# A hybrid attention layer on one core: the order of small work at four joints, and a last row block in column halves

## Chip, core and metric

One NeuronCore of a Trainium2 chip runs the whole layer. The metric is the device time of one execution in microseconds, from runs on the chip; shorter is better.

## The reference, cut to what matters

A single encoder layer in float32 over 1024 tokens of width 1024: a half-step SwiGLU, attention, and a second half-step SwiGLU, each between two RMS norms. One projection gives q, k and v; eight heads attend over a two-dimensional neighbourhood, eight over a mixture of dilated windows; each group is normalised and the two go through one output matrix.

```
h = swiglu(rmsnorm(x, ffn1_pre_g[l]), ffn1_w_gate[l], ffn1_w_up[l], ffn1_w_down[l])
x = x + 0.5 * rmsnorm(h, ffn1_post_g[l])
h = rmsnorm(x, mix_pre_g[l])
qkv = (h @ w_qkv[l]).reshape(B, S, 3, N_HEADS, HEAD_DIM).transpose(2, 0, 3, 1, 4)
...
o_na = rmsnorm(o_na.transpose(0, 2, 1, 3).reshape(B, S, D_NA), na_out_g[l])
o_dil = rmsnorm(o_dil.transpose(0, 2, 1, 3).reshape(B, S, D_DIL), dil_out_g[l])
mixed = jnp.concatenate([o_na, o_dil], axis=-1) @ w_out[l]
x = x + rmsnorm(mixed, mix_post_g[l])
h = swiglu(rmsnorm(x, ffn2_pre_g[l]), ffn2_w_gate[l], ffn2_w_up[l], ffn2_w_down[l])
x = x + 0.5 * rmsnorm(h, ffn2_post_g[l])
```

## The kernel before, in words

**Arithmetic.** Every large product is made from high and low parts of both factors: ScalarE casts a high part, VectorE subtracts it to get the low part, and TensorE does three matmuls (high by high, high by low, low by high). The feed-forward products and the q, k and v projections go by a seven-product scheme over halves of the matrices (`PASSES`, line 31), in which a pass may go on accumulating in the banks of the pass before it (`CHAINED`, line 32).

**What sets the order.** The program writes TensorE's order out by hand. Small work of the other engines is handed out in between. `c.todo` is a queue of closures of which one is popped at each `c.tick()`, and `c.steps` and `c.sums` are queues of which one entry each is popped at each `c.step()`, which stands every few matmuls. `plan(n, {i: [...]})` fills `c.todo` with n ticks and what is to run at each. `c.behind(f, engine)` places what f issues behind the latest instruction of that engine. Apart from such ties, VectorE and ScalarE are put into an order when the program is built, by what is ready and by the order in which it was written. On the chip every engine runs its own list strictly in order.

**Row blocks.** The 1024 tokens are eight blocks of 128 rows, t = 0 to 7, of which 0 to 3 and 4 to 7 are the two halves of the scheme. `fin.rest` adds the normalised result of a sub-layer to x (line 892), stores x and hands the block to `op.norm`, which takes squares on ScalarE (`sumsq`, line 166), a reciprocal root on VectorE (`rstd_of`, lines 149 to 159) and a scaling (line 230). `op.put(t)` transposes a block on TensorE (line 174) and builds the scheme's operands from it (`left_half`, `right_half`, lines 290 to 319).

**The values joint.** `vp.run(0, 1)` does two passes of the value projection in twelve ticks: eight of two chunks for one row block each, then four of four chunks. The plan for it has blocks 4 and 5 at tick 0, the transposes of block 4 at tick 8 and blocks 6 and 7 at tick 10. After it `pg.ahead` starts the q and k projection: product of pair 0, a copy of it out of its bank (`save` and `keep`, line 488), product of pair 1, then a second product of pair 0 on top of the first in the same bank.

**The local heads.** Eight neighbourhood heads (`na_head`) of eight steps each follow the eight dilated heads, with a tick at every second step. In their first ticks the last pair of dilated heads is finished. `merge` (line 1255) reads `obn`, which comes back from memory, weighs two partial results on VectorE, has GpSimd multiply (lines 1281 and 1282) and VectorE add (line 1285). Then `attended` (line 1862), which only the last pair has as its `then`, queues the norm of the dilated rows: squares, root, scaling (line 1390) and transposes into the operand of the output projection, and between them `begin`, which puts matmuls of the output projection between the steps of the heads.

**The output joint.** After the last head, the norm of the neighbourhood rows is finished and they are transposed, eight blocks in two quads, among sixteen matmul groups: a closure of `puts` after the groups 2, 3, 5, 6, 9, 10, 12 and 13. `GroupNorm.put` (line 1392) makes four transposes (line 1401) into one of two banks, and for each of two strips a cast on ScalarE (line 1405) and a subtraction on VectorE (line 1406).

**The tail.** In the last pass of the last feed-forward layer eleven chunks are added up for the row blocks 4 to 7 in turn (line 793). `combine` adds the bank to what is kept (line 830), `Finish.half` takes the squares and multiplies by the gain (line 850), `Finish.end` makes the root (lines 864 to 867 and `newton`, lines 322 to 329) and adds the scaled result to x in two halves (line 871), one stored from SP's queue and one from ScalarE's (line 872). The right halves of these blocks are complete one pass earlier.

Of the kernel before, what the change touches and what calls it, by code (L numbers as in the profile page):

```python
# [22 lines left out]
EPS = 1e-6  # L23
# [706 lines left out]
class Passes:  # L730
# [4 lines left out]
    def __init__(self, c, n, left, right, take, last=None):  # L735
        self.c, self.left, self.right, self.take = c, left, right, take
        self.own = not isinstance(left, Operand)
        groups = [list(range(i, min(i + 4, n))) for i in range(0, n, 4)]
        self.groups = [groups] * 6 + [last or groups]
        self.groups[0] = [groups[0][:2], groups[0][2:]] + groups[1:]  # L740
        self.todo = deque((p, g[j:j + 2]) for p in range(7) for g in self.groups[p] for j in range(0, len(g), 2))
        self.ready = deque()
# [27 lines left out]
    def run(self, *which, upto=6):  # L770

        c = self.c
        for p in which:
# [4 lines left out]
            for gi, g in enumerate(groups):  # L778
                self.fetched(len(g) + 1, upto)
                ops = [self.ready.popleft() for _ in g]  # L780
                end = gi == len(groups) - 1
                for t in range(4):
                    if t == 1:
                        self.fetched(3, upto)
                    if acc[t] is None:
                        acc[t] = c.psm.tile([P, T], F32, tag="mm", name="accp")
                    sl = slice(t * P, (t + 1) * P)
                    n = 2 if t == 0 else 1
                    for j in range(0, len(ops), n):
                        two = [(a[:, sl], b) for i in (0, 1, 2) for (ahi, alo), (bhi, blo) in ops[j:j + n]  # L790
                               for a, b in [((ahi, bhi), (alo, bhi), (ahi, blo))[i]]]
                        for i, (a, b) in enumerate(two):
                            c.nc.tensor.matmul(acc[t], a, b, start=not chained and gi == 0 and j == i == 0,  # L793
                                               stop=end and j + n >= len(ops) and i == len(two) - 1,
                                               skip_group_check=chained)
                        if n == 2 or j % 2:
                            c.step()
                    if end:
                        self.take(p, t, acc[t])
                    c.tick()  # L800


def combine(c, halves, rows):
# [7 lines left out]
    def take(p, t, ps):  # L811
# [17 lines left out]
        else:  # L829
            nc.vector.tensor_add(c21[:, t], ps, c21[:, t])  # L830
            halves(4 + t, 0, c21[:, t])
            rows(4 + t, second[:, t])
    return take


class Finish:


    def __init__(self, c, src, dst, gain, op, last=False):
        self.c, self.src, self.dst, self.gain, self.op, self.last = c, src, dst, gain, op, last  # L840
        self.ss = c.small.tile([P, 8, 2], F32, tag="fss", name="fss", bufs=1)
        self.xs = {}

    def half(self, t, g, h):

        sumsq(self.c, h, self.ss[:, t, g:g + 1])
        to = h
        if self.last and t >= 4 and g == 0:
            to = self.part = self.c.xp.tile([P, T], F32, tag="hm", name="hm")
        self.c.nc.vector.tensor_mul(to, h, self.gain[:, g * T:(g + 1) * T])  # L850

    def load(self):
# [4 lines left out]
        self.q = c.small.tile([P, 4], F32, tag="q", name="q", bufs=1)  # L857
        c.behind(lambda: c.nc.scalar.activation(self.q[:, 0:1], c.ident[:, :1], AF.Sqrt), ACT)

    def end(self, t, h):  # L860

        c, nc = self.c, self.c.nc
        x, q = self.xt[t - 4], self.q[:, t - 4:t - 3]
        nc.vector.tensor_scalar(q, self.ss[:, t, 1:2], 0.5 / D, 0.5 * EPS, op0=ALU.mult, op1=ALU.add)
# [4 lines left out]
        for g, queue in enumerate((nc.sync, nc.scalar)):  # L869
            sl = slice(g * T, g * T + T)  # L870
            nc.vector.scalar_tensor_tensor(x[:, sl], h[:, sl] if g else self.part, r, x[:, sl], op0=ALU.mult, op1=ALU.add)  # L871
            queue.dma_start(self.dst[t][:, sl], x[:, sl])
# [238 lines left out]
class DilPair:  # L1111
# [97 lines left out]
    def outs(self, hd, part, quad, un, pt, po):  # L1209
# [30 lines left out]
        if (hd, part, quad) == (1, 0, 1):  # L1240
            c.todo.extend([lambda: None] + [lambda: c.behind(self.merge, DVE, ACT)])
# [13 lines left out]
    def merge(self):  # L1255
# [100 lines left out]
class GroupNorm:  # L1356
# [35 lines left out]
    def put(self, i):  # L1392
# [7 lines left out]
        for j in range(4):  # L1400
            nc.tensor.transpose(ps[:, j, :], o[:, j * P:(j + 1) * P], c.ident)
        for hf in range(2):
# [3 lines left out]
            nc.vector.tensor_sub(lo, src, hi.bitcast(F32))  # L1406


def layer(tc, a, out):
    nc = tc.nc  # L1410
    c = Ctx(tc)
    with ExitStack() as ctx:
# [81 lines left out]
        def ffn(which, op, prep, pg, get, turns, sums, more, post, pre, src, dst, begin=None, tables=()):  # L1494
# [60 lines left out]
            ps.take = combine(c, fin.half, rows)  # L1555
# [70 lines left out]
        with ExitStack() as order:  # L1626
# [142 lines left out]
            def vearly(p, t, ps):  # L1769
# [4 lines left out]
                else:  # L1774
# [9 lines left out]
                      9: [lambda: c.behind(lambda: pg.split_left(0), DVE, ACT)], 10: [A(6, 7)]})  # L1784
# [77 lines left out]
        def attended():  # L1862
# [14 lines left out]
            c.todo.extend(single + [scales[0], lambda: None] + puts[:4] + [begin] + squares + [scales[1], lambda: None])  # L1877
# [18 lines left out]
        with ordered():  # L1896
# [159 lines left out]
```

## Time and profile before

| | us |
|---|---|
| three runs, median | 1828.5 |
| three runs, lowest to highest | 1827.25 to 1829.3 |
| the profiled execution, its own time | 1826.53 |
| the profiled execution, its span | 1824.7 |
| TensorE busy | 1807.9 |
| VectorE busy | 1308.9 |
| ScalarE busy | 831.6 |
| GpSimd busy | 348.8 |

The span runs from the first to the last instruction of the program on the core, and the time holds the 1.8 us around it. An engine counts as busy from the start of an instruction to its end. Matmuls overlap, so TensorE's busy time says little about how densely it works; the distance from one start to the next does. A bracket at the end of a row of a timeline holds the idle time before the instruction and what ended it.

### The profile page before, as it was taken

To read this page: it belongs to the slowest core of one execution; us is meant where nothing else is said; L and a number is where in the kernel's file an instruction comes from. 1 tells how busy PE (TensorE), PEld (TensorE's weight loads), DVE (VectorE), ACT (ScalarE), POOL (GpSimd) and SP (SyncE) were. 2 spreads that over 40 slices of the span, in tenths; PEclk is the share of its full clock that TensorE was granted. 3 is DMA by queue.
4 is the path that set the end of the run, shared out by engine and by line. 5 is a ranking of instruction groups with operands and counts; after the bars stand their busy time and mean duration, and the time that the engine had idled before them with its cause. 6 is when DMAs were issued, how large, how long until landed. Compare 5 with 4: busy or idle time off the path is not lost. (4 is left out here: it accounts for less than half of the span.)

```text
span 1824.7 us, 25161 instructions
## 1 busy us (share of the span) xinstructions
PE 1807.9 (99%) x8876; PEld 1521.7 (83%) x8876; DVE 1308.9 (72%) x2225; ACT 831.6 (46%) x1495; POOL 348.8 (19%) x579
## 2 busy tenths in 40 slices
PE   8999999999999999999999999999999999999998
PEld 6888888888888888888999998887888888888886
DVE  6888877776466877577676856778877777664557
ACT  7522233334534556234688765554223333354433
POOL 2124421112021123232344100221111111110000
PEclk9999999999999999999999999999999999999999
DMA  8756566557888867768687523594655566596564
GB/s 295 258 170 220 171 230 224 193 209 268 307 305 294 288 206 266 261 230 292 193 271 255 183 88 116 193 312 159 197 180 194 201 220 224 184 351 198 191 229 146
DMA packets 172769, 409.28 MB, mean 224 GB/s; under 512 B 20401, under 2 KB 42321, under 8 KB 170594
## 3 DMA queue, kind: packets, MB, share of 16 engines
q1 hardware_dynamic: 125168, 248.68, 41.5%
q0 software_dynamic: 46608, 157.41, 23.7%
q8 instruction: 70, 1.15, 0.3%
q10 hardware_dynamic: 866, 1.58, 0.2%
q14 instruction: 57, 0.47, 0.1%
HBM read 280.09 MB, written 132.56 MB: 226 GB/s over the span
## 5 line engine op out<-in xcount | busy, mean ns | idle before, releaser
L472 PE MATMUL mmp<-x,whi 128*128 128x512 f32 (+1 forms) x1464 | 571.7, 391 | 1.1 <-ACT x L181 0.7
L473 PE MATMUL mmp<-x,whi 128*128 128x512 f32 (+1 forms) x1464 | 569.1, 389 | 0.7 <-DVE x L182 0.7
L793 PE MATMUL accp<-pw 128*128 128x512 f32 x1800 | 411.1, 390 | 0.0
L793 PEld LDWEIGHTS accp<-pw 128*128 128x128 f32 x1800 | 337.2, 188 | 70.0 <-ACT hb L814 0.3
L478 PE MATMUL mmp<-x,wlo 128*128 128x512 f32 (+1 forms) x1464 | 390.5, 388 | 0.2 <-DVE wlo L463 0.2
L472 PEld LDWEIGHTS mmp<-x,whi 128*128 128x128 f32 x1464 | 275.7, 188 | 58.7 <-ACT s L488 1.4
L473 PEld LDWEIGHTS mmp<-x,whi 128*128 128x128 f32 x1464 | 275.7, 188 | 57.2 <-DVE x L182 1.4
L478 PEld LDWEIGHTS mmp<-x,wlo 128*128 128x128 f32 x1464 | 274.4, 188 | 57.4 <-DVE wlo L463 0.6
L761 DVE TENSOR_TENSOR pw<-praw,pw 128x1024 fp32r<-128x1024 f32 (+1 forms) x181 | 200.1, 1143 | 125.6 <-ACT pw L760 124.8
L760 ACT CAST pw<-praw 128x1024 fp32r<-128x1024 f32 (+1 forms) x181 | 168.7, 983 | 207.7 <-PE accp L793 167.3
L462 ACT CAST whi<-wraw 128x1024 fp32r<-128x1024 f32 x126 | 132.6, 1053 | 187.4 <-PE mmp L473 157.9
L463 DVE TENSOR_TENSOR wlo<-wraw,whi 128x1024 fp32r<-128x1024 f32 x126 | 153.9, 1222 | 2.9 <-ACT whi L462 2.9
L703 POOL DMA_DIRECT2D g<-sg x44 | 23.9, 544 | 427.6 <-DVE sg L696 246.5
L462 ACT CAST whi<-traw 128x512 fp32r<-128x512 f32 x52 | 32.3, 621 | 122.6 <-DVE traw L564 89.7
L488 ACT COPY s<-mmp 128x512 f32<-128x512 f32 x49 | 28.8, 588 | 127.7 <-PE mmp L478 121.1
L655 DVE TENSOR_TENSOR c<-mmp,u 128x512 f32<-128x512 f32 x52 | 35.9, 691 | 70.9 <-PE mmp L478 70.7
L563 DVE TENSOR_TENSOR wraw<-wraw 128x1024 f32<-128x1024 f32 x52 | 63.6, 1224 | 17.7 <-DMA wraw<-in_wu_dram 17.0
L793 PE MATMUL accp<-pw,x 128*128 128x512 f32 x312 | 71.8, 390 | 0.0
L1095 DVE CUSTOM_DVE_ANT_0 s<-sp,g 128x256 f32<-128x256 f32 (+1 forms) x128 | 48.4, 413 | 30.7 <-PE sp L1192 24.6
L793 PEld LDWEIGHTS accp<-pw,x 128*128 128x128 f32 x312 | 58.3, 188 | 12.4 <-DVE pw L761 0.3
L642 DVE TENSOR_TENSOR c<-mmp,v 128x512 f32<-128x512 f32 x52 | 35.8, 689 | 34.0 <-PE mmp L478 34.0
L1341 PE MATMUL po<-vs,pt 128*128 128x128 f32 x352 | 49.9, 276 | 0.4 <-DVE pt L1107 0.4
(281 smaller groups left out, 2485.7 us busy)
## 6 DMA issues: line engine op xcount, KB each, us to landing
praw<-g SPq DMA_DIRECT2D x70, 512.0 KB
wraw<-in_wg_dram SPq DMA_DIRECT2D x44, 512.0 KB
wraw<-in_wu_dram SPq DMA_DIRECT2D x44, 512.0 KB
tr<-in_wd_dram SPq DMA_DIRECT2D x44, 512.0 KB
g<-sg POOLq DMA_DIRECT2D x88, 256.0 KB, 5.4
ts<-tr POOLq DMA_DIRECT2D x22, 1024.0 KB, 4.7
praw<-ts SPq DMA_DIRECT2D x88, 256.0 KB
praw<-in_wd_dram SPq DMA_DIRECT2D x66, 256.0 KB
```

Of the source, the lines that this page charges most:

```text
L462: nc.scalar.copy(hi, raw)
L463: nc.vector.tensor_sub(lo, raw, hi.bitcast(F32))
L472: mm(out, hi[:, i, sl], xhi[:, k, cols], start=not go_on and k == 0, stop=False, skip_group_check=go_on)
L473: mm(out, hi[:, i, sl], xlo[:, k, cols], start=False, stop=False, skip_group_check=go_on)
L478: mm(out, lo[:, i, sl], xhi[:, k, cols], start=False, stop=k == 3, skip_group_check=go_on)
L563: nc.vector.tensor_sub(r[:, 0:2], r[:, 1:3], r[:, 0:2])
L655: c.behind(lambda: nc.vector.tensor_add(c21, d, u2), *((DVE,) if self.sink.soon and b == self.n - 1 else ()))
L760: nc.scalar.copy(hi, raw[:, :m])
L761: nc.vector.tensor_sub(lo, raw[:, :m], hi.bitcast(F32))
L793: c.nc.tensor.matmul(acc[t], a, b, start=not chained and gi == 0 and j == i == 0, stop=end and j + n >= len(ops) and i == len(two) - 1, sk ...
L1095: c.nc.vector.tensor_tensor_reduce(out=s, in0=ps, in1=bias, scale=-1.0, scalar=3e38, op0=ALU.add, op1=ALU.min, accum_out=neg)
L1341: nc.tensor.matmul(po[0][:, u], pt[0][:, j, :], vs[:, k0 + j, :], start=j == 0, stop=j == n - 1)
```

## The change

The change has five parts.

1. In the plan of the values joint, blocks 6 and 7 go from tick 10 to tick 7.
2. For the last pair of dilated heads, `merge` is queued behind two empty ticks instead of one, and `attended` runs in the tick of the sum instead of the tick after it.
3. In `attended` an empty tick is put between the root of the first quad and its first transposes.
4. In `GroupNorm.put` with strips, both casts of a block come ahead of both subtractions; in the output joint the root of the second quad is issued ahead of the first block's transposes instead of behind them.
5. In the last pass, block 7 takes its last two chunks apart from the others. The long part is added to what is kept as before; then six matmuls of 256 columns give the left half of the rest in a bank of its own, and six more the right half. Each half is added, squared and multiplied by the gain as it comes, and the left half's mean joins the right half's mean of the pass before, as a bias (`q`) of the square root. For blocks 4 to 7 the square root reads the sum of squares directly, and the Newton step is written as one fused operation between two reciprocals. Block 7's gain products for the left half and for the third quarter of the columns lie in PSUM. VectorE scales and adds these three quarters, and GpSimd does the last quarter with a product and a sum, stored from SP's queue.

```diff
+                    tail = self.tail if end and p == 6 and t == 3 and self.tail else None
+                    rest = ops[-2:] if tail else []
+                    ops = ops[:len(ops) - len(rest)]
...
+                    for i in range(2 if tail else 0):
+                        ps, cols = c.psm.tile([P, T], F32, tag="mm", name="accq")[:, :T // 2], slice(i * T // 2, (i + 1) * T // 2)
+                        six = [(x[:, sl], y[:, cols]) for k in (0, 1, 2) for (ahi, alo), (bhi, blo) in rest
+                               for x, y in [((ahi, bhi), (alo, bhi), (ahi, blo))[k]]]
+                        for k, (x, y) in enumerate(six):
+                            c.nc.tensor.matmul(ps, x, y, start=k == 0, stop=k == len(six) - 1)
+                        tail(i, cols, ps)
...
+    def tail(i, cols, ps):
+        h = c21[:, 3, cols]
+        c.behind(lambda: nc.vector.tensor_add(h, ps, h), DVE)
+        halves(7, -i, h)
+        if i:
+            rows(7, second[:, 3])
...
+        elif g == 1:
+            sumsq(c, h, self.ss[:, 7, 1:2])
+            self.right = c.pst.tile([P, 4, P], F32, tag="tr", name="hr").rearrange("p k x -> p (k x)")[:, :H]
+            mul(self.right, h[:, :H], self.gain[:, T:T + H])
+            mul(h[:, H:], h[:, H:], self.gain[:, T + H:])
+            self.centre(7)
+        else:
+            if g:
+                self.mean(7, 0)
+            else:
+                self.part = c.pst.tile([P, 4, P], F32, tag="tr", name="hl").rearrange("p k x -> p (k x)")
+            cols = slice(-g * H, (1 - g) * H)
+            sumsq(c, h, self.ss[:, 4 if g else 7, 0:1])
+            mul(self.part[:, cols], h, self.gain[:, cols])
...
-        nc.vector.scalar_tensor_tensor(v, self.ss[:, t, 0:1], 0.5 / D, q, op0=ALU.mult, op1=ALU.add)
-        nc.scalar.activation(e, v, AF.Sqrt, scale=2.0)
-        r = newton(c, y, e, v)
...
+        nc.scalar.activation(e, ss, AF.Sqrt, scale=0.25 / D, bias=q)
+        nc.vector.scalar_tensor_tensor(v, ss, 0.25 / D, q, op0=ALU.mult, op1=ALU.add)
+        nc.vector.reciprocal(y, e)
+        nc.vector.scalar_tensor_tensor(e, v, y, e, op0=ALU.mult, op1=ALU.add)
+        nc.vector.reciprocal(y, e)
...
+        out(nc.sync, slice(0, T), self.part)
+        if t < 7:
+            out(nc.scalar, slice(T, D), h[:, T:])
+            return
+        m = T + T // 2
+        out(nc.scalar, slice(T, m), self.right)
+        nc.gpsimd.tensor_mul(h[:, m:], h[:, m:], y.broadcast_to([P, D - m]))
+        nc.gpsimd.tensor_add(x[:, m:], h[:, m:], x[:, m:])
+        nc.sync.dma_start(self.dst[t][:, m:], x[:, m:])
...
-            c.todo.extend([lambda: None] + [lambda: c.behind(self.merge, DVE, ACT)])
+            c.todo.extend([lambda: None] * (2 if self.then else 1) + [lambda: c.behind(self.merge, DVE, ACT)])
...
-        c.todo.extendleft(([self.then] if self.then else []) + [lambda: c.behind(add, DVE), lambda: None,
-                          lambda: c.behind(products, POOL)] + ([] if self.then else [lambda: None]))
+
+        def added():
+            c.behind(add, DVE)
+            if self.then:
+                self.then()
+        c.todo.extendleft([added, lambda: None, lambda: c.behind(products, POOL)] +
+                          ([] if self.then else [lambda: None]))
...
+        lows = []
         for hf in range(2):
...
             nc.scalar.copy(hi, src)
-            nc.vector.tensor_sub(lo, src, hi.bitcast(F32))
+            lows.append((lo, src, hi.bitcast(F32)))
+        for args in lows:
+            nc.vector.tensor_sub(*args)
...
-                      9: [lambda: c.behind(lambda: pg.split_left(0), DVE, ACT)], 10: [A(6, 7)]})
+                      9: [lambda: c.behind(lambda: pg.split_left(0), DVE, ACT)], 7: [A(6, 7)]})
...
-            c.todo.extend(single + [scales[0], lambda: None] + puts[:4] + [begin] + squares + [scales[1], lambda: None])
+            c.todo.extend(single + [scales[0], lambda: None, lambda: None] + puts[:4] + [begin] + squares + [scales[1], lambda: None])
...
-                        puts.append(lambda n=n: (n.put(0), c.behind(lambda: early[1].scale(2), DVE)))
+                        puts.append(lambda n=n: (c.behind(lambda: early[1].scale(2), DVE), n.put(0)))
```

## Rows read from the trace of the kernel before

**Rows 1.** The profile's page, part 1: busy time by engine.

```profile
PE 1807.9 (99%) x8876; PEld 1521.7 (83%) x8876; DVE 1308.9 (72%) x2225; ACT 831.6 (46%) x1495; POOL 348.8 (19%) x579
```

**Rows 2.** The waits of TensorE, whole span: us in total, times, longest.

```profile
PE gps L350 <- DMA xn<-in_ffn_pre_g_dram: 5.6, 1, 5.6
...
PE trp L1401 <- DVE og L1390: 0.4, 1, 0.4
PE trp L174 <- DVE og L1390: 0.4, 1, 0.4
PE po L1341 <- DVE pt L1107: 0.4, 1, 0.4
```

**Rows 3.** Groups of instructions by line and shape: busy us, mean ns, idle before.

```profile
L793 PE MATMUL accp<-pw 128*128 128x512 f32 x1800 | 411.1, 390 | 0.0
...
L1406 DVE TENSOR_TENSOR n<-trp,n 128x256 fp32r<-128x256 f32 x16 | 6.5, 421 | 1.9 <-ACT n L1405 1.9
...
L128 POOL TENSOR_TENSOR wlo<-wraw,whi 128x256 fp32r<-128x256 f32 x16 | 11.6, 729 | 17.1 <-ACT whi L127 17.1
```

**Rows 4.** Timeline, TensorE and ScalarE at 679 to 684 us: start, length, instruction.

```profile
678.95 1.07 PE L478 MATMUL mmp<-x,wlo 128*128 128x512 f32 x4
...
680.77 0.60 PE L174 MATMUL trp<-ident,x 128*128 128x128 f32 x4
681.12 0.48 PE L472 MATMUL mmp<-x,whi 128*128 128x512 f32 x1
...
683.06 0.60 PE L174 MATMUL trp<-ident,x 128*128 128x128 f32 x4
683.78 0.50 PE L472 MATMUL mmp<-x,whi 128*128 128x512 f32 x1
...
681.62 1.06 ACT L166 ACTIVATE junk<-x 128x1024 bf16<-128x1024 f32 x1
...
683.14 0.59 ACT L488 COPY s<-mmp 128x512 f32<-128x512 f32 x1
```

**Rows 5.** Timeline, TensorE and VectorE at 1009 to 1012 us.

```profile
1011.63 0.94 PE L1341 MATMUL po<-vs,pt 128*128 128x128 f32 x6 [0.40 <-DVE pt L1107]
...
1009.48 0.18 DVE L1261 TENSOR_TENSOR mn<-sa,obn 128x16 f32<-128x16 f32 x1 [0.95 <-DMA obn<-rg]
```

**Rows 6.** Timeline, TensorE at 1037 us.

```profile
1036.77 0.63 PE L174 MATMUL trp<-ident,og 128*128 128x128 f32 x4 [0.42 <-DVE og L1390]
```

**Rows 7.** Timeline, TensorE, VectorE and ScalarE at 1112 to 1119 us.

```profile
1113.34 0.40 PE L365 MATMUL accp<-whi,o 128*128 128x512 f32 x1
1113.82 0.63 PE L1401 MATMUL trp<-ident,og 128*128 128x128 f32 x4
...
1118.21 0.63 PE L1401 MATMUL trp<-ident,og 128*128 128x128 f32 x4 [0.43 <-DVE og L1390]
...
1113.60 0.15 DVE L147 TENSOR_TENSOR v<-gss 128x4 f32<-128x4 f32 x1
...
1112.85 0.65 ACT L1405 CAST n<-trp 128x256 fp32r<-128x256 f32 x2 [1.23 <-DVE n L1406]
```

**Rows 8.** Timeline, the end: VectorE and the issue of the last store.

```profile
1816.02 0.75 DVE L871 SCALAR_TENSOR_TENSOR xl<-hb,y,xl 128x512 f32<-128x512 f32 x1
...
1817.35 0.69 DVE L830 TENSOR_TENSOR hb<-accp,hb 128x512 f32<-128x512 f32 x1 [0.59 <-PE accp L793]
...
1818.89 0.16 DVE L866 SCALAR_TENSOR_TENSOR v<-fss,q 128x1 f32<-128x1 f32 x1
...
1819.91 0.16 DVE L328 SCALAR_TENSOR_TENSOR y<-e,y 128x1 f32<-128x1 f32 x1
...
1821.55 0.34 ACTq L872 DMA_DIRECT2D out_dram<-xl  x1
```

**Rows 9.** Timeline, TensorE at 20 us: matmuls of 256 columns.

```profile
19.88 0.64 PE L478 MATMUL mmp<-x,wlo 128*128 128x256 f32 x4
20.35 0.28 PE L472 MATMUL mmp<-x,whi 128*128 128x256 f32 x1
```

More of the change, by code (lines that the diff above doesn't have):

```diff
@@ L740, in __init__ @@
         self.groups[0] = [groups[0][:2], groups[0][2:]] + groups[1:]
+        self.tail = None
         self.todo = deque((p, g[j:j + 2]) for p in range(7) for g in self.groups[p] for j in range(0, len(g), 2))
@@ L799, in run, with combine @@
                         self.take(p, t, acc[t])
+                    for i in range(2 if tail else 0):
[5 more added lines that the diff above has]
+                        tail(i, cols, ps)
                     c.tick()
-def combine(c, halves, rows):
+def combine(c, halves, rows, split=False):
     nc = c.nc
@@ L830, in take @@
             nc.vector.tensor_add(c21[:, t], ps, c21[:, t])
+            if split and t == 3:
+                return
             halves(4 + t, 0, c21[:, t])
             rows(4 + t, second[:, t])
-    return take
+    def tail(i, cols, ps):
[4 more added lines that the diff above has]
+            rows(7, second[:, 3])
+    return (take, tail) if split else take
 class Finish:
@@ L841, in __init__, with mean @@
         self.ss = c.small.tile([P, 8, 2], F32, tag="fss", name="fss", bufs=1)
+        if last:
+            self.q = c.small.tile([P, 4], F32, tag="q", name="q", bufs=1)
         self.xs = {}
     def half(self, t, g, h):
[L846 to L850, printed above, removed]
+        c, nc, H = self.c, self.c.nc, T // 2
+        mul = nc.vector.tensor_mul
+        if not (self.last and t == 7):
+            sumsq(c, h, self.ss[:, t, g:g + 1])
+            to = h
+            if self.last and t >= 4 and g == 0:
+                to = self.part = c.xp.tile([P, T], F32, tag="hm", name="hm")
+            mul(to, h, self.gain[:, g * T:(g + 1) * T])
+        elif g == 1:
[12 more added lines that the diff above has]
+            mul(self.part[:, cols], h, self.gain[:, cols])
+    def mean(self, t, i):
+        q = self.q[:, t - 4:t - 3]
+        self.c.nc.vector.scalar_tensor_tensor(q, self.ss[:, t, i:i + 1], 0.25 / D, q, op0=ALU.mult, op1=ALU.add)
     def load(self):
@@ L856, in load @@
             c.nc.sync.dma_start(self.xt[t], self.src[4 + t])
-        self.q = c.small.tile([P, 4], F32, tag="q", name="q", bufs=1)
         c.behind(lambda: c.nc.scalar.activation(self.q[:, 0:1], c.ident[:, :1], AF.Sqrt), ACT)
@@ L862, in end, with out, centre @@
         c, nc = self.c, self.c.nc
-        x, q = self.xt[t - 4], self.q[:, t - 4:t - 3]
-        nc.vector.tensor_scalar(q, self.ss[:, t, 1:2], 0.5 / D, 0.5 * EPS, op0=ALU.mult, op1=ALU.add)
-        v, y, e = [c.small.tile([P, 4], F32, tag=i, name=i)[:, :1] for i in ("v", "y", "e")]
-        nc.vector.scalar_tensor_tensor(v, self.ss[:, t, 0:1], 0.5 / D, q, op0=ALU.mult, op1=ALU.add)
-        nc.scalar.activation(e, v, AF.Sqrt, scale=2.0)
-        r = newton(c, y, e, v)
[L869 to L872, printed above, removed]
+        x, q, ss = self.xt[t - 4], self.q[:, t - 4:t - 3], self.ss[:, t, 0:1]
+        if t < 7:
+            self.centre(t)
+        else:
+            ss = self.ss[:, 4, 0:1]
+        v, y, e = [c.small.tile([P, 4], F32, tag=i, name=i)[:, :1] for i in ("v", "y", "e")]
+        nc.scalar.activation(e, ss, AF.Sqrt, scale=0.25 / D, bias=q)
[3 more added lines that the diff above has]
+        nc.vector.reciprocal(y, e)
+        def out(queue, cols, src):
+            nc.vector.scalar_tensor_tensor(x[:, cols], src, y, x[:, cols], op0=ALU.mult, op1=ALU.add)
+            queue.dma_start(self.dst[t][:, cols], x[:, cols])
+        out(nc.sync, slice(0, T), self.part)
+        if t < 7:
+            out(nc.scalar, slice(T, D), h[:, T:])
+            return
+        m = T + T // 2
[3 more added lines that the diff above has]
+        nc.sync.dma_start(self.dst[t][:, m:], x[:, m:])
+    def centre(self, t):
+        self.c.nc.vector.tensor_scalar(self.q[:, t - 4:t - 3], self.ss[:, t, 1:2], 0.25 / D, 0.25 * EPS,
+                                       op0=ALU.mult, op1=ALU.add)
     def scale(self, t0, n):
@@ L1554, in rows @@
                     fin.end(t, hs[t])
-            ps.take = combine(c, fin.half, rows)
+            if pre is None:
+                ps.take, ps.tail = combine(c, fin.half, rows, True)
+            else:
+                ps.take = combine(c, fin.half, rows)
             if masks:
```

## The prediction

> **What bounds the kernel now.** I read the busy times first: TensorE is busy 99% of the span, VectorE 72%, the others less [rows 1]. No other engine can be the bound as a whole, so the change can win only where TensorE stands still, and after its last matmul. Second, the list of TensorE's waits [rows 2]: 5.6 us before its first matmul, which the change does not touch, and then three single waits of 0.4 us, each on VectorE. Third, how tightly the matmuls follow one another: 1800 of 512 columns cover 411.1 us, one each 0.228 us, while one takes 0.390 us from start to end [rows 3]. So a matmul normally starts 0.16 us before its predecessor ends. A gap that the profile shows as 0.40 us therefore costs 0.56 us, and a wait of up to 0.16 us shows no gap at all. Fourth, the timelines around those waits and at the end.
>
> These rows limit the matter before any detail: three waits of under 0.6 us, a few hidden ones, and an end in which 4.2 us pass from the last product's first use (1817.35) to the issue of the last store (1821.55) [rows 8]. Over 4 us cannot well come of it, and 0.2% of the time, about what a measurement of this kernel can tell from no change, is 3.7 us.
>
> **Part 1: rows 6 and 7 normalised three ticks earlier (value projection).** In `pg.ahead` the second projection of pair 0 accumulates on top of the first, so it must wait until ScalarE has copied the first out (L488). The bank was complete at 680.0, where the four low-part matmuls end, yet the copy runs only at 683.14 to 683.73, because ScalarE is in the two squares of x rows 6 and 7 (the second ends at 682.7). Four transposes are normally followed by a matmul 0.35 us after they start (680.77 to 681.12); here it takes 0.72 (683.06 to 683.78) [rows 4]. The stall is 0.37 us. From tick 7 the squares are released during the second pass instead, before this copy is due. Everything they bring moves with them: two additions, two stores of x on GpSimd's queue, the root (12 small VectorE operations), the scaling of row 6. The loads and additions have no tie and are ready either way; I cost their move at nothing, since the values pass has no TensorE wait in rows 2 that would show them as late. What is behind the moved work is the split of row 4's sums. Its last step frees the buffer that row 5's copy needs, in ScalarE's queue ahead of L488. I take 0.30 saved. Ends: 0.37 saved, and up to 3.8 us lost (rival 4).
>
> **Part 2: the last merge one tick later.** VectorE reaches the merge at 1009.48 after standing 0.95 us for the load of `obn`; the softmax operations and the copy of the transposed weights queue behind it, and TensorE then waits 0.40 us for that copy [rows 5], so 0.56 us. Two no-ops instead of one move the merge back by one tick, two of the local head's eight steps, and the load has landed by then. The merge's own small operations still cost what they cost, but without a blocked queue. GpSimd's products move one tick later with it; the sum and `attended` fall together into the tick in which `attended` ran, so the squares behind it do not move. I take 0.55 saved. Ends: 0.56 saved; 0.3 lost, if sum and merge meet a fuller stretch of VectorE.
>
> **Part 3: one more no-op ahead of the first transposes of the dilated rows.** At 1036.77 TensorE waits 0.42 us for VectorE's scaling of `og` [rows 6], 0.58 us in all. One tick later that scaling is long done. All following transposes and the filler matmuls also move one tick; their number is unchanged, and fillers only stand elsewhere. I take 0.58 saved. Ends: 0.58 and 0.3, if a filler lands badly.
>
> **Part 4: the output joint.** Two edits act together. The root for the second quad now goes to VectorE before the first transposed block is split: so far its first operation starts at 1113.60, after that split, and TensorE waits 0.43 us at 1118.21 for the row that it scales [rows 7]: 0.59 us. That first subtraction ended as ScalarE was released at 1112.85 and began 0.42 sooner; the root can take its place, about 1.2 us earlier. And both ScalarE copies of a block now precede both VectorE subtractions. So far the second copy waits for the first subtraction: ScalarE idles 1.23 us before it, released by VectorE. That holds the transposes' bank: the third block's transposes start 0.48 us after the matmul before them instead of 0.24 [rows 7], a hidden wait of 0.24. Against it: the subtractions of the first block now share VectorE with the root, which can hold the same bank longer. I take the 0.59 and two thirds of the 0.24: 0.75 saved. Ends: 1.1 (a few tenths more of hidden waits at the later blocks) and nothing.
>
> **Part 5: the tail.** Step by step from the last rows [rows 8]:
> - Matmuls: the last two chunks are six of 512 columns, 6 x 0.228 = 1.37 us; now twelve of 256. Four of these start within 0.47 us (19.88 to 20.35), 0.118 each, and one lasts 0.28 [rows 9]: 1.41 us, and the last one drains 0.11 us sooner. TensorE ends about where it did; the left half is done 0.7 us sooner.
> - VectorE: the addition of the long part is ready 1.4 us before the end, but the engine is in the end of row block 6 until 1816.77 [rows 8]. Block 6's root loses two dependent steps of about 0.2 us (v before the square root, one Newton step), so it is free near 1816.37. Then 0.69 (long addition), and with 256-column operations of 0.42 [rows 3] the left addition, left product and right addition follow, overlapping a little: the right half is ready at about 1818.25. Square and accumulator took the 0.85 us from 1818.04 to 1818.89 at 512 columns; at half, between 0.43 and 0.85, I take 0.55: 1818.80, only 0.1 sooner than now.
> - Root: square root (0.2), reciprocal, one fused step, reciprocal, each 0.2 apart (five steps from 1818.89 to 1819.91 now): y at about 1819.6, against 1820.07 (1819.91 + 0.16).
> - Scaling: VectorE lets go of the left half after 0.67 (its scalings of 512 columns last 0.75 and overlap a little) and needs under 0.5 for a quarter, ready for the ScalarE queue at 1820.8. GpSimd needs two operations of 128x256. The nearest row is 0.729 each [rows 3]: 1819.65 + 1.46 = 1821.1, and SP's queue, whose left-half store was issued at about 1820.4, is free. The last issue is near 1821.15, now 1821.55.
>
> By the GPSIMD Reference of the Trainium skill (section 4.1, engine selection) element-wise work belongs on VectorE, GpSimd being about twice as slow with two inputs. By that, an estimate, each would take 0.84 and the tail would save 0.2; no run here shows that ratio at this size, and the measured 0.729 is used.
>
> I take 0.4 saved; the smaller last transfer is counted as nothing. Ends: 0.8 (GpSimd as fast as VectorE) and 0.7 lost (rival 1). The extra work on block 7's right half one pass earlier (two products of 0.42 instead of one of 0.69, one small step) stands beside TensorE's matmuls, with no wait of TensorE there in rows 2.
>
> **Sum.** 0.30 + 0.55 + 0.58 + 0.75 + 0.4 = 2.6 us. The profiled execution took 1826.5 us (span 1824.7), so 1823.9 for one like it; it was 2.0 us below the median of the three runs, and against that median, 1828.5, the forecast is 1825.9.
>
> **Rivals.**
> 1. *GpSimd sets the end.* If its two operations run only after VectorE's scalings (1820.8), the last store is issued at 1820.8 + 1.46 = 1822.3, 0.7 later than now: the sum is 2.2 - 0.7 = 1.5 saved, 1827.0. For it: both read the same tiles from the same moment. Against: the products that VectorE scales now lie in PSUM. The page SBUF — State Buffer of the Trainium skill (Who interferes with whom) says that a VectorE instruction with two SBUF inputs and a GpSimd one that reads SBUF shut each other out; by it there is no clash here, and no row before shows the pair. Chance 0.12.
> 2. *The stalls move.* VectorE is 72% busy overall [rows 1], so a cured wait may return as the next late copy; if half of parts 1 to 4 comes back, 1.1 + 0.4 = 1.5 saved, 1827.0. The hidden waits (no gap below 0.16 us) speak for it, the fact that each shown wait has one plain cause against. Chance 0.17.
> 3. *All at its best end*: 0.37 + 0.56 + 0.58 + 1.1 + 0.8 = 3.4, and with a shorter last transfer near 3.8: 1824.7. Chance 0.13.
> 4. *Slower: row 6's root ahead of row 4's split.* Twelve steps 0.2 apart and a scaling of 1024 columns (twice the 0.67 to 0.75 of 512) enter VectorE's queue ahead of the last splits of row 4; if all 3.8 us reach the buffer that row 5's copy waits for, ScalarE's copies behind it and TensorE stand for it: 2.3 - 3.8 = 1.5 lost, 1830.0. It decides as soon as the delay exceeds the 2.3 us of the other parts. Against: VectorE is not full, so some of it falls into gaps, and the same work stood behind those splits before. Chance 0.06.
> 5. *No effect on the order*: VectorE and ScalarE are ordered when the kernel is built, and ticks may not change what they do; then only part 3 and the tail count, 1.0 saved, 1827.5. Chance 0.05.
>
> The forecast has the remaining 0.47.
>
> **How the numbers follow.** The range must hold the cases but for 2 in 10, and the three runs before lay 2 us apart: 1823.9 to 1828.2. Faster by over 0.2% (below 1824.8) takes rival 3 and the upper edge of the forecast: 0.18. Slower by over 0.2% would take a stall in the profile that I do not see, or rival 4 and more: 0.03. Within 0.2%: 0.79.
>
> **What would show it.** Right: the three waits of 0.4 us gone from TensorE's list; the copy of pair 0 near 680; no 0.95 us before the merge; the last issue 0.4 us nearer to the last matmul. Wrong: a new wait of TensorE at the values joint, or after the output joint's first block; GpSimd's two operations starting after VectorE's; a TensorE gap between the two halves at the end.

## The result, and the profile after

The change makes the kernel slower: 1833.1 us (median of 10 runs, 1828.2 to 1834.7) against 1828.0 us (10 runs, 1824.3 to 1831.3) of the kernel before. The ratio is 1.0032, 95% interval 1.0024 to 1.0040, so 5.9 us (4.4 to 7.3) by the ratio and 5.1 us by the medians. The forecast was 1825.9 us with a range up to 1828.2. The profiled execution of after took 1833.6 us (span 1831.8), 7.1 us over that of before.

The waits of TensorE come first, as in [rows 2] and without the 5.6 us at the start, which are the same. Line numbers differ in the kernel after: the transposes of the output joint are L1468 (were L1401), the subtractions L1476 (L1406), the scalings of `og` L1457 (L1390).

```profile
PE trp L1468 <- DVE n L1476: 3.7, 1, 3.7
PE mmp L478 <- DVE wlo L463: 1.2, 1, 1.2
PE po L1287 <- ACT pt L1169: 1.0, 1, 1.0
...
PE po L1408 <- ACT pt L1169: 0.2, 1, 0.2
```

The three waits of 0.4 us are gone, as forecast. In their place stand one of 3.7 us at the output joint (part 4) and one of 1.2 us at the values joint (part 1). The third, L1287, is in dilated heads that no edit touches. The last, L1408, is in the local heads and new as well (run 4).

TensorE's ledger: from the starts of successive matmuls, I took by how much each distance exceeds the regular one of its size (0.227 us for 512 columns, 0.175 for 384, 0.12 for 256, 0.11 for 128) and summed it by stretch; below this is called the excess. In us, for four kernels whose runs are described here and below:

| stretch (us of the span) | before | after | after, again | best combination |
|---|---|---|---|---|
| start, to 27 | 7.9 | 8.8 | 7.9 | 7.9 |
| values joint, 672 to 730 | 0.8 | 2.0 | 2.2 | 0.8 |
| dilated heads, 850 to 1000 | 2.9 | 4.7 | 3.1 | 3.9 |
| local heads, 1000 to 1098 | 3.2 | 2.4 | 2.4 | 2.4 |
| output joint, 1098 to 1128 | 1.5 | 5.8 | 5.8 | 0.8 |
| 1128 to 1300 | 2.9 | 2.2 | 3.2 | 1.2 |
| all stretches | 18.2 | 24.7 | 23.5 | 16.0 |
| TensorE's end to the span's end | 7.4 | 7.9 | 7.9 | 7.3 |

The last sum takes in the rest of the span, where the distances lie 1.0 to 1.2 us under the regular ones in all four. After against before this makes 6.5 + 0.5 = 7.0 us, the whole difference of the spans. Of it 2.7 us (start, dilated heads) are not the change's: the second profile of the same kernel has them at 0.0 and 0.2. The output joint alone is 4.3 us in both.

**Output joint.** Timeline of the kernel after, TensorE, VectorE and ScalarE at 1114 to 1125 us, which answers to [rows 7]:

```profile
1116.33 0.40 PE L365 MATMUL accp<-whi,o 128*128 128x512 f32 x1
1120.40 0.63 PE L1468 MATMUL trp<-ident,og 128*128 128x128 f32 x4 [3.67 <-DVE n L1476]
...
1123.52 0.63 PE L365 MATMUL accp<-whi,o 128*128 128x512 f32 x1
...
1115.59 0.16 DVE L147 TENSOR_TENSOR v<-gss 128x4 f32<-128x4 f32 x1
...
1117.98 0.16 DVE L159 SCALAR_TENSOR_TENSOR y<-e,y 128x4 f32<-128x4 f32 x1
1118.18 1.41 DVE L1457 SCALAR_TENSOR_TENSOR og<-og,y,gd 128x512 f32<-128x512 f32 x2
1119.51 1.41 DVE L1476 TENSOR_TENSOR n<-trp,n 128x256 fp32r<-128x256 f32 x4
...
1114.24 0.65 ACT L1473 CAST n<-trp 128x256 fp32r<-128x256 f32 x2 [3.30 <-PE trp L1468]
1115.37 0.65 ACT L1473 CAST n<-trp 128x256 fp32r<-128x256 f32 x2 [0.49 <-PE trp L1468]
```

Both copies of the first block are done at 1114.89, before VectorE comes to the first step of the root at 1115.59; its subtractions could have stood there. They run at 1119.51, 3.92 us later: VectorE takes its list in order, and thirteen steps of the root, 0.2 us apart (1115.59 to 1118.18), and two scalings (1.33 us) stand ahead of them, all before the first subtraction of either block. The third block's transposes need the first block's bank, so TensorE stands for 3.67 us. In the kernel before, the root's first step stands behind the first block's split [rows 7], and its other steps alternate with the subtractions of the next blocks, as here:

```profile
1114.52 0.42 DVE L1406 TENSOR_TENSOR n<-trp,n 128x256 fp32r<-128x256 f32 x1
1114.86 0.15 DVE L157 TENSOR_TENSOR e<-y,v 128x4 f32<-128x4 f32 x1
```

**Clock.** Behind the standstill a matmul of 512 columns takes 0.63 us instead of 0.40. The stretches of the kernel after (a row has the stretch, its length, the busy time of each engine, PEclk, which is the granted clock, and the DMA's share and rate; 0.50 is the lower level, 1.2 of 2.4 GHz):

```profile
1112.00:1116.00 4.00, 4.00 (x23) 3.35 (x22) 3.69 (x16) 1.28 (x4) 0.00 (x0) 1.00 0.00 0
1116.00:1120.30 4.30, 0.73 (x4) 0.25 (x2) 3.92 (x16) 0.02 (x1) 0.00 (x0) 1.00 0.00 0
1120.30:1122.00 1.70, 1.60 (x8) 1.30 (x9) 0.87 (x3) 0.65 (x2) 0.00 (x0) 0.78 0.00 0
1122.00:1124.00 2.00, 2.00 (x9) 1.71 (x8) 0.92 (x4) 0.65 (x2) 0.00 (x0) 0.50 0.00 0
1124.00:1126.00 2.00, 2.00 (x10) 1.64 (x9) 1.00 (x3) 0.00 (x0) 0.00 (x0) 0.83 0.00 0
```

Of the joint's 5.8 us, 3.84 are the gap itself (1116.33 to 1120.40, less 0.227). The matmuls started from 1121.10 to 1124.74 take 3.64 us, and the same ones in the best combination 2.05, so the low level costs 1.6 us. Another 0.8 us is there without the root first too (best combination), less 0.4 for the wait for `og`, which after does not have.

**Values joint.** Timeline of the kernel after, VectorE, TensorE and ScalarE at 673 to 685 us, against [rows 4]:

```profile
673.59 0.17 DVE L149 TENSOR_SCALAR v<-ss 128x2 f32<-128x2 f32 x1 [0.91 <-ACT junk L166]
...
678.35 0.15 DVE L159 SCALAR_TENSOR_TENSOR y<-e,y 128x2 f32<-128x2 f32 x1
...
679.55 1.28 DVE L230 SCALAR_TENSOR_TENSOR x<-x,y,gain 128x1024 f32<-128x1024 f32 x1
680.75 2.49 DVE L305 TENSOR_TENSOR x<-s,x 128x512 fp32r<-128x512 f32 x4
683.16 1.22 DVE L463 TENSOR_TENSOR wlo<-graw,whi 128x1024 fp32r<-128x1024 f32 x1
...
684.43 1.20 PE L478 MATMUL mmp<-x,wlo 128*128 128x512 f32 x4 [1.22 <-DVE wlo L463]
...
683.33 0.58 ACT L290 COPY s<-trp 128x512 f32<-128x512 f32 x1 [2.59 <-DVE x L305]
683.81 0.59 ACT L488 COPY s<-mmp 128x512 f32<-128x512 f32 x1
```

The root of rows 6 and 7 and the scaling of row 6 push row 4's splits (L305) back, and behind those the low part of the weights for pair 1, for which TensorE waits. ScalarE is free of the squares, but stands 2.59 us for the same splits ahead of row 5's copy (L290), so that the copy of pair 0 (L488) runs at 683.81, not near 680.

**Tail.** Timeline of the kernel after from TensorE's end (1823.91), which answers to [rows 8]:

```profile
1823.39 0.52 PE L809 MATMUL accq<-pw 128*128 128x256 f32 x3
...
1826.34 0.16 DVE L916 RECIPROCAL y<-e 128x1 f32<-128x1 f32 x1
1826.54 0.75 DVE L919 SCALAR_TENSOR_TENSOR xl<-hl,y,xl 128x512 f32<-128x512 f32 x1
1826.73 0.61 POOL L927 TENSOR_TENSOR hb<-hb,y 128x256 f32<-128x256 f32 x1 [38.14 <-DVE y L916]
...
1827.41 0.72 POOL L928 TENSOR_TENSOR xl<-hb,xl 128x256 f32<-128x256 f32 x1
...
1828.16 0.33 SPq L929 DMA_DIRECT2D out_dram<-xl  x1
1828.59 0.40 SPq L920 DMA_DIRECT2D out_dram<-xl  x1
```

The left half is scaled by 1827.3 (1826.54 + 0.75), but its store (L920 on SP) goes out at 1828.59, behind the one that waits for GpSimd (L929). The last issue ends 5.1 us after TensorE's end; before it was 4.6 us.

### The profile page after: what moved, and what is told of

The parts are those of the page before. It is cut to its first block, busy times and chain, and to the rows that moved or that the text cites. A ratio compares the mean times of both kernels' runs of the same rounds, so it can differ in the third digit from the quotient of the medians.

```text
span 1831.8 us, 25188 instructions
## 1 busy us (share of the span) xinstructions
PE 1810.0 (99%) x8882; PEld 1525.0 (83%) x8882; DVE 1310.8 (72%) x2226; ACT 831.9 (45%) x1497; POOL 349.0 (19%) x581
## 5 line engine op out<-in xcount | busy, mean ns | idle before, releaser
L463 DVE TENSOR_TENSOR wlo<-wraw,whi 128x1024 fp32r<-128x1024 f32 x126 | 153.2, 1217 | 2.8 <-ACT whi L462 2.8
L488 ACT COPY s<-mmp 128x512 f32<-128x512 f32 x49 | 28.8, 587 | 128.0 <-PE mmp L478 121.1
L1408 PE MATMUL po<-vs,pt 128*128 128x128 f32 x352 | 50.0, 276 | 0.4 <-ACT pt L1169 0.2
```

Source lines behind the costliest of these rows:

```text
L463: nc.vector.tensor_sub(lo, raw, hi.bitcast(F32))
L1408: nc.tensor.matmul(po[0][:, u], pt[0][:, j, :], vs[:, k0 + j, :], start=j == 0, stop=j == n - 1)
```

## The experiments

Each run stands against 29 to 33 runs of the kernel before on its own chip (medians 1828.4 us for runs 1 to 4, 1827.3 for 5 to 8, 1828.1 for 9 to 12). Runs 1 to 4 and 9 to 12 ran on one chip, 5 to 8 on another. Differences in us are the ratio's, times 1828.

**1. After without the root first.**

```diff
-puts.append(lambda n=n: (c.behind(lambda: early[1].scale(2), DVE), n.put(0)))
+puts.append(lambda n=n: (n.put(0), c.behind(lambda: early[1].scale(2), DVE)))
```

> The kernel after, but the root for the second quad stands behind the split of the first transposed block again, as in the kernel before; all other edits stay. Theory (root first): root and both scalings stand ahead of the first subtractions on VectorE and hold the banks of both transposed blocks, so without it TensorE's wait of 3.67 us for L1476 goes, the matmuls behind it no longer run at the lower clock level, and the time falls by 3.5 to 5 us against the kernel after, to about 1828 or 1829 on the median of the kernel before. Rival (both casts first): the order of casts and subtractions holds the banks, the wait of 3 to 4 us stays, and the time stays within 1 us of the kernel after.

1827.05 us, ratio 0.9993 (0.9984 to 1.0001). The wait is gone, the joint's excess falls from 5.8 to 0.8 us. This single line holds the loss. The times give 7 us between this ratio and the first one of after, each uncertain by some 1.5, the rows 5.0 us. Against run 10, the kernel after on this run's chip, it is 5.3 us by the ratios and 4.6 by the medians, which fits the rows.

**2. Before with the root first, and nothing else** (the same line the other way round).

> The kernel before with one edit: the root for the second quad ahead of the split of the first transposed block. Casts and subtractions alternate as before. Theory (root first): 3.5 to 5 us slower than the kernel before, with one wait of TensorE of 3 to 4 us at the transposes of the third block, on VectorE's subtraction, and matmuls behind it that last about 0.6 us instead of 0.4. Rival (both casts first): no wait over 0.5 us there, the time within 0.6 us of the kernel before or 0.6 us faster.

1832.81 us, ratio 1.0028 (1.0017 to 1.0039): 5.1 us slower (3.1 to 7.1). Its timeline, VectorE and TensorE:

```profile
1118.19 0.16 DVE L159 SCALAR_TENSOR_TENSOR y<-e,y 128x4 f32<-128x4 f32 x1
1118.27 0.41 DVE L1406 TENSOR_TENSOR n<-trp,n 128x256 fp32r<-128x256 f32 x1
1118.60 1.40 DVE L1390 SCALAR_TENSOR_TENSOR og<-og,y,gd 128x512 f32<-128x512 f32 x2
1119.92 0.74 DVE L1406 TENSOR_TENSOR n<-trp,n 128x256 fp32r<-128x256 f32 x2
...
1120.48 1.09 PE L1401 MATMUL trp<-ident,og 128*128 128x128 f32 x4 [3.52 <-DVE n L1406]
```

One subtraction slips in ahead of the scalings, but a bank is free only when both are done, so the wait is nearly the same. The rival, that the casts hold the banks, is out: here they alternate as before.

**3. Before with rows 6 and 7 from tick 7** (`10: [A(6, 7)]` becomes `7: [A(6, 7)]`).

> The kernel before with one edit: rows 6 and 7 are normalised from tick 7 of the value projection instead of tick 10. Theory: about 1.1 us slower; the copy of pair 0 is early, but the root and the scaling of rows 6 and 7 delay the low part of the weights of pair 1, for which TensorE waits about 1.2 us. Rival (the forecast's part 1): 0.3 us faster, no TensorE wait over 0.4 us between 675 and 700 us.

1828.12 us, ratio 0.9999 (0.9990 to 1.0008). The trace has the wait (0.9 us for `wlo` L463; 1.8 us of excess against 0.8), the times can't tell it from nothing. Run 12 asks again.

**4. Before with the two edits of the local heads** (the merge one tick later, the empty tick ahead of the dilated rows' transposes).

> The kernel before with the two edits of the local heads: the last merge one tick later, and one more step without work ahead of the first transposes of the dilated rows. Theory: 0.7 to 1.1 us faster; TensorE's waits of 0.40 and 0.42 us between 1000 and 1040 us are gone and VectorE does not stand 0.95 us for the load of obn. Rival (the stalls move): other copies of the same heads come late, and the time is within 0.3 us of the kernel before.

1826.22 us, ratio 0.9984 (0.9975 to 0.9993): 2.9 us faster (1.3 to 4.6). Both waits are gone. More came of it than expected, and the seven profiles in which the merge stands where it stood before say why. In each VectorE waits for the load of `obn`, and TensorE behind it; the extremes are [rows 5] and this one, of run 6:

```profile
1011.22 0.18 DVE L1323 TENSOR_TENSOR mn<-sa,obn 128x16 f32<-128x16 f32 x1 [2.77 <-DMA obn<-rg]
...
1013.37 1.65 PE L1403 MATMUL po<-vs,pt 128*128 128x128 f32 x6 [2.22 <-DVE pt L1169]
```

VectorE's wait was 0.95, 1.08, 1.30, 1.43, 1.51, 2.36 and 2.77 us, TensorE's 0.40, 0.53, 0.75, 0.88, 0.96, 1.82 and 2.22: 1.1 on the mean. The profile that the forecast was read from has the smallest of the seven. The excess of the local heads is 3.2 to 6.2 us in these seven, 4.1 on the mean, and 2.4 in each of the seven profiles with both edits. Not all of the cure is kept: in all of those TensorE waits some 0.2 us at a new place for a copy of the transposed weights on ScalarE, the last row of the list of after above (in run 4 0.25 us at 1023.14). That distance is 0.41 us over the regular one, and another, 14 us later, 0.27.

**5. Before with both casts first.**

```diff
+lows = []
...
-nc.vector.tensor_sub(lo, src, hi.bitcast(F32))
+lows.append((lo, src, hi.bitcast(F32)))
+for args in lows:
+    nc.vector.tensor_sub(*args)
```

> The kernel before with one edit: at the output joint both ScalarE copies of a transposed block precede both VectorE subtractions; the root stays behind the first split. Theory: the scaling that TensorE waits 0.43 us for comes earlier and the copies no longer alternate, so TensorE's time over its pitch between 1098 and 1128 us falls from 1.5 to about 0.8 us, and the time by 0.5 to 0.8 us. Rival (this edit holds the banks): a TensorE wait of 1 us or more on a subtraction, 1 to 4 us slower.

1825.74 us, ratio 0.9991 (0.9982 to 0.9999): 1.6 us faster (0.2 to 3.3). The joint's excess is 0.77 us instead of 1.54, and TensorE's wait for the scaling 0.19 us instead of 0.43:

```profile
1119.38 0.63 PE L1401 MATMUL trp<-ident,og 128*128 128x128 f32 x4 [0.19 <-DVE og L1390]
```

The rest of that 0.77 us comes from distances too short to show a gap.

**6 to 8. Three tails.** Run 6 is before with the tail of the change alone; run 7 puts the stores in order; run 8 takes GpSimd out.

```diff
-nc.sync.dma_start(self.dst[t][:, m:], x[:, m:])
+c.behind(lambda: nc.sync.dma_start(self.dst[t][:, m:], x[:, m:]), SP)
...
-nc.gpsimd.tensor_mul(h[:, m:], h[:, m:], y.broadcast_to([P, D - m]))
-nc.gpsimd.tensor_add(x[:, m:], h[:, m:], x[:, m:])
-nc.sync.dma_start(self.dst[t][:, m:], x[:, m:])
+out(nc.sync, slice(m, D), h[:, m:])
```

> The kernel before with the whole tail of the change and nothing else. Theory: SyncE's queue holds the left half's store behind the store that waits for GpSimd, so the last issue comes 5.0 to 5.2 us after TensorE's end where it was 4.6, and the time is 0.3 to 0.7 us longer. Rival (the forecast's part 5): 0.4 us shorter, last issue 4.2 us after TensorE's end.

> The tail alone as in the run before this one, with one edit: the store of GpSimd's quarter stands behind the store of the left half in SyncE's list. Theory: the left half's store is issued about 0.9 us earlier, GpSimd's store ends the kernel, issued 4.4 to 4.7 us after TensorE's end, 0.4 to 0.7 us earlier than with the tail alone. Rival (GpSimd, not the queue, sets the end): GpSimd's two operations end at the same time and the last issue moves by less than 0.2 us.

> The tail alone, but VectorE scales the last quarter too, and GpSimd has no part in it. Theory (GpSimd is late even with a free queue): VectorE's third scaling of 0.3 to 0.5 us ends before GpSimd's 1.3 us would, and the last issue comes 4.0 to 4.4 us after TensorE's end, the shortest of the three tails. Rival: VectorE's own order (block 6's root, additions) is the bound, and the last issue is within 0.2 us of the tail with the stores in order.

Ratios: 1.0000 (0.9991 to 1.0009), 0.9997 (0.9988 to 1.0006), 0.9998 (0.9990 to 1.0007). No tail can be told from the old one in time. In the traces the end of the last issue lies 5.06, 4.57 and 4.51 us behind TensorE's end, 4.57 in the kernel before. Run 7, with TensorE's end at 1820.17:

```profile
1822.59 0.16 DVE L916 RECIPROCAL y<-e 128x1 f32<-128x1 f32 x1
...
1823.56 0.33 SPq L920 DMA_DIRECT2D out_dram<-xl  x1
...
1824.41 0.33 SPq L929 DMA_DIRECT2D out_dram<-xl  x1
```

So the order on SP's queue cost 0.5 us. With it mended, GpSimd's quarter and VectorE's third scaling come out alike, and the last issue is no earlier than in the old tail: `y` is ready only 0.17 us earlier than before. Run 8 is the shortest of the three, but misses its 4.0 to 4.4; its rival, within 0.2 us of run 7, is what came. The span ends 7.2 us behind TensorE's end in runs 7 and 8, and 7.3 to 7.5 in the five profiles with the old tail (before and runs 2 to 5). That is 0.1 to 0.3 us, which the times don't show; that it comes of the shorter last store is likely, but not tested.

**9. After, with only the small steps of the root first.**

```diff
-puts.append(lambda n=n: (c.behind(lambda: early[1].scale(2), DVE), n.put(0)))
+puts.append(lambda n=n: (c.behind(lambda: early[1].scale(0), DVE), n.put(0),
+                         c.behind(lambda: [early[1].scaled(k) for k in range(2)], DVE)))
```

> The kernel after, with one edit: only the thirteen small steps of the root for the second quad stand ahead of the first block's split; its two scalings stand behind that split. Theory (a block of work ahead of the subtractions holds the banks, and its length is the wait): without the two scalings, 1.33 us in the trace, the first subtractions come 1.3 us earlier, TensorE's wait at the third transposes falls from 3.7 to about 2.3 us, and the time by 1.3 to 2.3 us against the kernel after (the upper end if the low clock level behind the wait shortens too). Rival (any root first costs the same, through the order of the list): wait and time as in the kernel after, within 0.5 us.

The wait follows the length of the work ahead, as expected: 2.20 us.

```profile
1117.19 0.16 DVE L159 SCALAR_TENSOR_TENSOR y<-e,y 128x4 f32<-128x4 f32 x1
1117.27 0.76 DVE L1476 TENSOR_TENSOR n<-trp,n 128x256 fp32r<-128x256 f32 x2
1117.94 1.40 DVE L1457 SCALAR_TENSOR_TENSOR og<-og,y,gd 128x512 f32<-128x512 f32 x2
...
1118.17 0.63 PE L1468 MATMUL trp<-ident,og 128*128 128x128 f32 x4 [2.20 <-DVE n L1476]
...
1120.15 0.63 PE L1468 MATMUL trp<-ident,og 128*128 128x128 f32 x4 [0.66 <-DVE n L1476]
```

The scalings now hold the second block's bank (0.66 us). The joint's excess is 3.65 us, 2.2 less than after. The time says it less clearly: 1830.99 us, ratio 1.0018 (1.0008 to 1.0028), against run 10's 1.0022, a gain of 0.6 us where 1.3 to 2.3 was expected, with overlapping intervals.

**10. The kernel after again**, on the chip of runs 1 to 4, 9, 11 and 12.

> The kernel after as it is, on the same chip as the three runs beside it, so that their differences are not taken across chips. Theory: 4 to 6 us slower than the kernel before, TensorE's wait of 3.5 to 3.8 us on VectorE's subtraction again. Rival (a part of the 5 us lay in loads that landed late in the first profile): within 3 us of the kernel before.

1831.63 us, ratio 1.0022 (1.0012 to 1.0031): 4.0 us slower (2.2 to 5.7), at the lower end of what was expected, the joint's wait 3.6 us.

**11. The best of the parts**: before with runs 4, 5 and 8 together.

> The kernel before with what the runs so far left standing: both edits of the local heads, both casts first at the output joint (the root behind the first split), the tail with VectorE scaling its last quarter; rows 6 and 7 from tick 10 as before. Theory (the parts add): heads 2.0 to 2.9, casts 0.7 to 1.5, tail 0 to 0.2, together 2.7 to 4.5 us faster than the kernel before. Rival (a cured wait comes back as the next late copy): under 1.5 us faster.

1825.21 us, ratio 0.9983 (0.9974 to 0.9992): 3.1 us faster than before (1.5 to 4.8), and 6.4 us faster than after on the medians beside it. It beats both kernels.

**12. The same with rows 6 and 7 from tick 7.**

> The run before this one with rows 6 and 7 from tick 7. Theory (the profiles): TensorE waits 0.9 to 1.2 us for the low part of the weights of pair 1, which the earlier tick puts behind root and scaling on VectorE; with tick 10 the seven profiles show 0.1 to 1.3 us over the pitch there, 0.4 on the mean; so 0.5 to 1.0 us slower than the run before this one. Rival (the time of the tick alone): within 0.4 us of it or faster.

1826.16 us, ratio 0.9991 (0.9982 to 1.0000): 0.95 us above run 11 on the medians, inside the expected 0.5 to 1.0. Eleven times against eleven, the means lie 1.0 us apart, with a 95% interval of 0.2 to 1.8. Its trace has the wait, run 11's has none:

```profile
683.73 1.21 PE L478 MATMUL mmp<-x,wlo 128*128 128x512 f32 x4 [0.94 <-DVE wlo L463]
```

## Why the prediction was wrong

The rows are differences of TensorE's excess, or for part 5 of the end of the span against TensorE's end; the times are differences of the runs. All in us.

| part | forecast | rows | times |
|---|---|---|---|
| 1, tick 7 | -0.30 | +0.8 to +1.7, +1.2 on the mean of all profiles | +0.95 (12 against 11); -0.2 ± 1.6 (3) |
| 2 and 3, local heads | -1.13 | -0.9 against the profile before, -1.7 against the mean of seven | -2.9 (-4.6 to -1.3) |
| 4, root first | part of -0.75 | +5.0 to +5.4 | +5.1 (3.1 to 7.1) |
| 4, casts first | part of -0.75 | -0.77 | -1.6 (-3.3 to -0.2) |
| 5, tail | -0.4 | +0.4 to +0.5 | 0.0 ± 1.6 |

**Part 4 is the step that failed.** It saw the very mechanism ("the root, which can hold the same bank longer") and then priced it at its best: "the root can take its place, about 1.2 us earlier", with "nothing" as the bad end. That counted the root as steps that slip in between, as they stand in the trace before. Issued first, they are one block in VectorE's list: 13 x 0.2 + 1.33 = 3.9 us ahead of the subtractions, and TensorE waited 3.67. Both terms of that sum were to be had from the trace before. The 1.6 us of low clock behind the wait were not: the clock is at its full level all through this joint in the trace before. Runs 1 and 2 show it from both sides, run 9 with a shorter block. The wait that the root was to cure was cured by the casts alone, nearly (0.43 to 0.19 us); that they alone gave the 0.77 us which the forecast took for both edits together (0.75) is luck.

**No bound in the text caught it.** "Over 4 us cannot well come of it" bounds the gain by the waits that are there; a loss isn't bounded by them. (The list of waits is longer than the forecast read it, too: beside the 5.6 us and the three of 0.4 it has 1.4 us on the operand `x` and a few of 0.2 and 0.3 us.) The slower rival was looked for at the values joint alone, so that slower by over 0.2% got a chance of 0.03. With the bad end of part 4 at nearly 4 us, the range would have reached past 1830, still short of the 1833.1 measured. Both new waits stand among its signs of being wrong, but only the one at the values joint had a price and a chance.

**Part 1** failed in sign, along its own bad end. Rival 4 named the place, row 4's splits behind the root, and its route through ScalarE's copies is there (2.59 us in after), but did not bind: the weights' low part behind the splits came later still for TensorE. The price was 0.8 to 1.7 us, not 3.8. The squares fell where ScalarE was free, as forecast, but the copy of pair 0 came only 0.2 us earlier (683.81 in after, where TensorE is 0.9 us later as the joint begins, against 683.14), since row 5's copy ahead of it waits for the splits. So the squares were not the only thing that held that copy, and that the stall of 0.37 us is gone altogether owes something to TensorE's own delay. On the time this rests on runs 11 and 12 and on the rows of the six profiles with tick 7, each with a wait of 0.9 to 1.3 us for `wlo`. The eight profiles with tick 10 are not alike either: their excess at this joint is 0.4 to 1.8 us, 0.9 on the mean, against 1.6 to 2.5, 2.1 on the mean.

**Parts 2 and 3** were right in mechanism; the term was too small. The wait for `obn` is a landing time that differs from run to run, and the profile read was the kindest of seven. By their mean, part 2 is worth 1.1 + 0.16 us instead of 0.55, together with part 3 1.8, less what comes back at the new place. The profile before also lay 2.0 us under its median, which the forecast noted and then only added back as an offset.

**Part 5**: the operations took about what was forecast (GpSimd 0.61 and 0.72 us against 0.729), and rival 1's condition did not come: GpSimd ran beside VectorE's scalings, which read PSUM. The GPSIMD Engine Reference of the Trainium skill (section 4.1, engine selection) has GpSimd about twice as slow as VectorE with two inputs; here it is 0.61 to 0.72 us against 0.42, so 1.5 to 1.7 times, and [rows 3] had 0.729 against 0.421 already. What failed is "SP's queue ... is free": the left half's store stands in that queue behind the store that waits for GpSimd. And `y` came 2.6 us after TensorE's end where the terms made 2.3, and GpSimd began 0.23 us behind it, where 0.05 was counted; with the queue in order (run 7) that leaves no gain at the last issue.

**Rival 2**, cured waits coming back, came in part, in the local heads: against the profile before, 0.56 and 0.58 us are gone and 0.41 and 0.27 us are new at other places (run 4), yet the stretch as a whole lost 0.9. At the output joint run 5 shows no new wait. The single parts of run 11 sum to 4.9 us (2.9 + 1.6 + 0.4) and gave 3.1; within the intervals, these agree.

**The sum.** Root first 5.0, tick 1.2, tail 0.5, casts -0.8 and local heads -0.9 to -1.7 make 4.2 to 5.0 us by the rows; the times of after gave 5.9 (4.4 to 7.3) and, again, 4.0 (2.2 to 5.7).

**Left open**: what makes the loads of the dilated heads land differently (excess of 2.7 to 4.7 us there in profiles of the same code), and the same of the load of `obn`.

## What to carry to other kernels

When a chain of small dependent steps is moved ahead of other work on an in-order engine, price it as one block: its whole length, plus what is issued with it, can become the wait of everybody who needs the work behind it. Ask for each queue what it holds back, the store queues too, and let the bad end of a reordering be that length, not zero. A wait on a DMA should be read from several executions before its removal is priced, since one profile may show the smallest of them.

## What the runs showed of the hardware

A standstill is not always paid in its own length alone. After TensorE, busy throughout until then, stood 3.67 us (after), 3.64 (run 10) and 3.52 (run 2), the granted clock was 0.50 for 3.4 us in the first two and for 6 us in run 2. Against the same matmuls at the full level that cost 1.6 us in the first two and 2.8 in run 2, whose stretches behind the standstill are:

```profile
1120.30:1122.00 1.70, 1.52 (x6) 1.45 (x7) 0.79 (x3) 0.75 (x2) 0.00 (x0) 0.50 0.00 0
1122.00:1124.00 2.00, 2.00 (x8) 1.60 (x8) 0.85 (x2) 0.63 (x2) 0.00 (x0) 0.50 0.00 0
1124.00:1126.00 2.00, 2.00 (x6) 1.58 (x5) 1.42 (x3) 0.48 (x2) 0.00 (x0) 0.50 0.00 0
```

A standstill of 2.2 us came out both ways: run 9 kept the full level, run 6 fell to the lower one. Run 9 and run 6, the stretches with the standstill and behind it:

```profile
1115.50:1118.10 2.60, 0.47 (x3) 0.04 (x1) 2.29 (x13) 0.00 (x0) 0.00 (x0) 1.00 0.00 0
1118.10:1120.10 2.00, 1.33 (x7) 0.88 (x7) 2.00 (x5) 0.65 (x2) 0.00 (x0) 1.00 0.00 0
```

```profile
1011.00:1014.00 3.00, 0.78 (x5) 0.63 (x4) 2.71 (x15) 1.68 (x6) 0.00 (x0) 0.88 0.15 57
1014.00:1016.00 2.00, 2.00 (x10) 1.90 (x10) 0.60 (x4) 0.71 (x2) 1.60 (x1) 0.50 0.03 8
```

So in these runs the gap's length alone does not tell whether the clock falls: four of the five standstills of 2.2 us or more in mid-kernel brought it down, and one did not.
